# An encoder layer on one core: the first MLP product by seven block products in place of eight

## The chip, the cores and the metric

The kernel runs on one core of a Trainium2 chip. The time is the device time of one execution in microseconds (us), and a version is timed by the median of its runs. PE is the matrix engine (its weight loads, PEld, overlap it), DVE the vector engine, ACT the scalar engine, POOL the general engine; SP issues most DMAs. SBUF is the on-chip memory, PSUM the eight banks into which PE writes.

## The reference

One encoder layer over 1536 tokens (1024 and 512, and 16 meta tokens) of width 1024. After attention, pooling and gates:

```python
x = layer_norm(DEEPNORM_ALPHA * x + mixed, ln1_g, ln1_b)
h = jnp.square(jax.nn.relu(x @ w_mlp1 + b_mlp1))
return layer_norm(DEEPNORM_ALPHA * x + (h @ w_mlp2 + b_mlp2), ln2_g, ln2_b)
```

`w_mlp1` is 1024 x 4096, `w_mlp2` 4096 x 1024, all in fp32. The first MLP product, `x @ w_mlp1`, is what the change computes in another way.

## The kernel before

**Precision.** Each operand of a product is split into a high part in the type fp32r (ACT, `hi`, L120) and the rest (DVE, `lo`, L123). One fp32 product is then three matmuls: high by high, high by rest, rest by high (`three`, L99 to L106; the matmul itself is L97 for the whole kernel). A weight block of 128 x 512 costs one ACT cast and one DVE subtraction.

**Groups.** The tokens are two groups g of 768 (`GN`; six tiles of 128, `GT`; two chunks of 384, `CH`). Phase 1 makes projections and attention. Phase 2 goes, for each group, through the branch projections (`p2`), `out_proj` (L981; PSUM banks added into the accumulator at L1002, statistics at L1003), `ln_N` (normalisation of the six tiles, ACT L193), `ln_T` (PE transposes L1025, ACT scale and shift L1028, split) and `mlp`. Group 0's `ln_T` runs beside group 1's `p2`; then come `out_proj(1)` and the MLPs of both groups.

**First MLP product** (`mlp1_unit`, L1048). A unit m is 128 of the 4096 hidden columns. For each chunk PE runs 8 k-blocks x 3 matmuls of 128x384 into one of six PSUM banks; then ACT takes bias and ReLU (L1060), DVE the square (L1061), ACT the high part, DVE the rest, into `hid`. PE waits for none of that at once: the next chunk has another bank.

**Second MLP product** (`mlp2_half`, L1073). After each four units come two halves of 512 output columns: per token tile 4 x 3 matmuls of 128x512, and one DVE addition to the accumulator (L1070). `residual2` (L1036) multiplies the accumulator by the LN1 row and adds a bias row (DVE L1041) in place. Each group has an accumulator of its own, `acc0` and `acc1`.

**Weights** come from DRAM by SP into three `rawp` buffers of 128x1024 (512 KB a load), are split into two `hlp` buffers, and each load waits until the splits of the buffer's earlier content are done.

**Start.** x is normalised by DVE (L305, L306) with two LN rows, which four small PE matmuls (`psr`) spread over the partitions and ACT copies (L273).

**Order.** The generators in `Background` interleave side work by ticks, one tick after each three matmuls of phase 2. A scheduler then sets the order of each engine's queue; an engine runs its queue strictly in that order, so an instruction that waits holds all behind it.

Of the kernel before, what the change touches and what calls it, by code (L numbers as in the profile page):

```python
# [76 lines left out]
class Trunk:  # L77
# [18 lines left out]
    def mm(self, out, st, mv, start, stop):  # L96
        self.nc.tensor.matmul(out, st, mv, start=start, stop=stop)  # L97

    def three(self, out, sh, sl, mh, ml, first, last, share_st=True):  # L99
        self.mm(out, sh, mh, first, False)  # L100
        self.mm(out, sh, ml, False, False)
        self.mm(out, sl, mh, False, last)
# [42 lines left out]
    def split(self, raw, hl, parts=2, n=D, dst0=0, eng=None):  # L145
        step = n // parts
        for i in range(parts):
            s = slice(i * step, (i + 1) * step)
            d = slice(dst0 + i * step, dst0 + (i + 1) * step)
            self.hi(hl[:, 0, d], raw[:, s])  # L150
            self.lo(hl[:, 1, d], raw[:, s], hl[:, 0, d], eng)
# [96 lines left out]
    def startup(self):  # L248
# [18 lines left out]
        def spread_row(r, n, sel):  # L267

            t = p0.tile([P, D], F32, name=f"row_{n}")
            for i in range(2):  # L270
# [2 lines left out]
                nc.scalar.copy(t[:, i * 512:(i + 1) * 512], ps)  # L273
# [1046 lines left out]
```

## Time and profile before

| | |
|---|---|
| three runs | 2206.4, 2207.15, 2208.91 us; median 2207.15 |
| the profiled execution | 2205.77 us, of which the span is 2204.0 |
| granted PE clock | 0.999 of full |
| PE, PEld | 2176.2 us (99%), 1931.6 us (88%) |
| DVE, ACT, POOL | 1228.2 us (56%), 804.9 us (37%), 155.6 us (7%) |
| first MLP matmul of group 0 | 1130.72 us from the start |

PE is busy when any matmul is in its pipeline. A group's mean time of one matmul (334 ns) is therefore longer than its share of the busy time (538.5 us / 3072 = 175 ns). "Idle before" is the engine's idle time ahead of an instruction, with what ended it.

### The profile page before, as it was taken

The numbers are of one execution on the slowest core, as the hardware profiler recorded it, in microseconds if no ns is written. First come the engines' busy times: TensorE is split into PE (matmuls) and PEld (weight loads), VectorE is DVE, ScalarE is ACT, GpSimd is POOL, SyncE is SP. The second block draws the span as 40 slices with busy tenths as digits, with TensorE's granted clock in tenths as the row PEclk, the third lists the DMA queues.
The fourth block names the chain that finished last, engine by engine and source line by source line (L and its number), as shares of the span: only waits on it lengthen the run. The fifth ranks groups of instructions, "written<-read, shape, count | busy, mean of one in ns | idle before, by whom it ended". The sixth has DMA issues, their size and how long they took to land.

```text
span 2204.0 us, 29394 instructions
## 1 busy us (share of the span) xinstructions
PE 2176.2 (99%) x11216; PEld 1931.6 (88%) x11216; DVE 1228.2 (56%) x2505; ACT 804.9 (37%) x1673; POOL 155.6 (7%) x222
## 2 busy tenths in 40 slices
PE   7999999999999999999999999999999999999998
PEld 6987789887887799799898999999989989989987
DVE  8436678767766536554664433433459443443447
ACT  3235656555554434333323322322332222222221
POOL 3100101101000022120000000000001000000001
PEclk9999999999999999999999999999999999999999
DMA  7342333323322447333323222221223312212211
GB/s 265 126 117 86 93 102 88 100 78 97 90 88 78 134 143 233 107 99 109 128 87 95 68 66 58 69 66 58 69 63 113 91 57 68 68 57 68 67 58 58
DMA packets 124377, 207.42 MB, mean 94 GB/s; under 512 B 23550, under 2 KB 78008, under 8 KB 124236
## 3 DMA queue, kind: packets, MB, share of 16 engines
q1 hardware_dynamic: 121644, 196.11, 29.3%
q0 software_dynamic: 2592, 9.44, 1.2%
q8 instruction: 88, 1.44, 0.3%
q14 instruction: 53, 0.43, 0.1%
HBM read 161.39 MB, written 44.11 MB: 93 GB/s over the span
## 4 chain that ended last, share of the span: by engine, by line
PE 65%; DVE 2%; DMA 1%; ACT 1%; POOL 0%; issue 0%; SPq 0%; DVEq 0%; POOLq 0%; ACTq 0%
PE m L97 48%; PE o L97 6%; PE ya L97 5%; PE psf L97 3%; PE yb L97 2%; PE pt L1025 0%; PE psw L97 0%; DMA gate<-GD 0%; DMA pw<-UT 0%; PE pso L97 0%; DMA oraw<-OT 0%; PE ptt L587 0%; DVE mlo L123 0%; DVE gate L964 0%; ACT S L561 0%
## 5 line engine op out<-in xcount | busy, mean ns | idle before, releaser
L97 PE MATMUL m<-L,hl_w 128*128 128x384 f32 x3072 | 538.5, 334 | 0.5 <-ACT hl_w L120 0.5
L97 PEld LDWEIGHTS m<-L,hl_w 128*128 128x128 f32 x3072 | 534.0, 188 | 3.3 <-ACT hl_w L120 0.9
L97 PE MATMUL m<-hl_w,hid 128*128 128x512 f32 x2304 | 533.6, 390 | 0.3 <-ACT m1f L1060 0.3
L97 PEld LDWEIGHTS m<-hl_w,hid 128*128 128x128 f32 x2304 | 430.5, 188 | 89.1 <-ACT m1f L1060 0.8
L97 PE MATMUL psf<-hT,hl_g 128*128 128x512 f32 x1152 | 306.1, 399 | 0.0
L120 ACT CAST hl_w<-raw_w 128x512 fp32r<-128x512 f32 x256 | 151.3, 619 | 368.1 <-issue 321.2
L1070 DVE TENSOR_TENSOR acc<-acc,m 128x512 f32<-128x512 f32 x192 | 131.3, 685 | 220.2 <-PE m L97 219.9
L97 PEld LDWEIGHTS psf<-hT,hl_g 128*128 128x128 f32 x1152 | 208.3, 189 | 34.1
L1061 DVE TENSOR_TENSOR m1f<-m1f 128x384 f32<-128x384 f32 x128 | 71.4, 559 | 271.4 <-ACT m1f L1060 271.4
L1060 ACT ACTIVATE m1f<-m,cols 128x384 f32<-128x384 f32 x128 | 74.4, 581 | 325.5 <-PE m L97 323.0
L123 DVE TENSOR_TENSOR hl_w<-raw_w,hl_w 128x512 fp32r<-128x512 f32 x256 | 170.4, 690 | 30.1 <-ACT hl_w L120 30.1
L97 PE MATMUL psf<-hT,hl_q 128*128 128x512 f32 x576 | 149.2, 397 | 0.0
L97 PE MATMUL ya<-L,hl_ba 128*128 128x384 f32 x768 | 138.1, 338 | 0.0
L97 PEld LDWEIGHTS ya<-L,hl_ba 128*128 128x128 f32 x768 | 133.6, 188 | 2.4
L561 ACT ACTIVATE S<-S,nm 128x400 f32<-128x400 f32 (+1 forms) x192 | 111.6, 583 | 44.6 <-DVE nm L557 44.5
L97 PE MATMUL o<-hl_wo,mhi 128*128 128x512 f32 x384 | 121.2, 397 | 2.3 <-DVE gate L963 2.1
L97 PEld LDWEIGHTS psf<-hT,hl_q 128*128 128x128 f32 x576 | 105.0, 189 | 17.7
L546 DVE CUSTOM_DVE_ANT_0 S<-pss,base 128x400 f32<-128x400 f32 (+1 forms) x192 | 96.7, 525 | 30.8 <-PE pss L97 30.0
L167 POOL TENSOR_TENSOR rs<-rs,nhalf 128x1 f32<-128x1 f32 (+1 forms) x25 | 34.7, 1388 | 1040.1 <-DVE rs L166 1040.1
L576 POOL TENSOR_SCALAR S<-S,rr 128x400 f32<-128x400 f32 (+1 forms) x96 | 57.3, 609 | 600.2 <-DVE pm L571 511.4
L120 ACT CAST pt<-ptt 128x512 fp32r<-128x512 f32 x128 | 71.4, 582 | 57.6 <-PE ptt L587 57.1
L97 PE MATMUL pss<-kst,qhl 128*128 128x400 f32 (+1 forms) x384 | 88.3, 329 | 1.1 <-DVE qhl L123 0.6
(156 smaller groups left out, 2460.0 us busy)
## 6 DMA issues: line engine op xcount, KB each, us to landing
raw_w<-w_mlp SPq DMA_DIRECT2D x128, 512.0 KB, 3.7
qraw<-QT SPq DMA_DIRECT2D x96, 128.0 KB, 2.7
GD<-eg SPq DMA_DIRECT2D x48, 256.0 KB, 2.3
gate<-GD SPq DMA_DIRECT2D x32, 384.0 KB, 3.1
raw_g<-w_in SPq DMA_DIRECT2D x16, 512.0 KB, 4.6
raw_ba<-w_bo_attn SPq DMA_DIRECT2D x16, 512.0 KB, 3.6
...
```

The costliest lines, as they stand in the source:

```text
L97: self.nc.tensor.matmul(out, st, mv, start=start, stop=stop)
L120: self.nc.scalar.copy(out, in_)
L123: (eng or self.nc.vector).tensor_tensor(out, x, f32(hi), op=ALU.subtract)
L167: self.nc.gpsimd.tensor_tensor(rs, rs, self.nhalf[:rs.shape[0]], op=ALU.pow)
L546: nc.vector.tensor_tensor_reduce(st.S[:, h, :st.n], ps[:, :st.n], self.base[:, st.var, st.o0:st.o0 + st.n], SLOPES[4 * st.j + h], -3.0e38, ...
L561: nc.scalar.activation(st.S[:, h, :st.n], st.S[:, h, :st.n], AF.Exp, bias=nm[:, h:h + 1], accum_out=den[:, h:h + 1])
L576: eng.tensor_scalar(st.S[:, h, :st.n], st.S[:, h, :st.n], rr[:, h:h + 1], 1.0, op0=ALU.mult, op1=ALU.mult)
L1060: nc.scalar.activation(f[:, :CH], ps[:, :CH], AF.Relu, bias=self.cols[:, C_BM1 + m:C_BM1 + m + 1])
L1061: nc.vector.tensor_tensor(f[:, :CH], f[:, :CH], f[:, :CH], op=ALU.mult)
L1070: self.nc.vector.tensor_tensor(ac, ac, ps, op=ALU.add)
```

## The change

**Seven products.** Units p and p+16 become a pair (`pair`). The 1024 input rows, the pair's 256 columns and the 768 tokens are each cut in two, and the 2x2 block product is made by the Winograd form of Strassen's scheme: seven products of 4 k-blocks x 3 matmuls of 128x384 in place of eight. They run in the order B11, T2, T3, T1, B21, T4, B22 into three PSUM banks a, b, c: a, b, c, b, a, c, b; a later product into a bank adds to what stands there. In between the bank is read: after B11 ACT copies a (p1); after T2 DVE makes u2 = b + p1, after T1 u4 = b + p1; then u4 += c (L1172) before T4 adds into c; after T4 u2 += c, and after B22 p1 += b. u4, u2, p1 and bank a (after B21) are the four output blocks; each gets ReLU and square on ACT, and the split.

**Weights of the products** (`w1_ops`). Four of the seven blocks are the weights or combinations of them, made in place in the raw buffers by DVE (s1 = a21 + a22 at L1122, and three more operations), and each of the seven is split into one of four half-size `hlp` buffers. After each product one further split is issued, four products ahead, into the buffer of the product that just ended. The last split of a pair reads the raw buffer of unit p; the load of the next pair's second unit (p+17) goes into that buffer. The second product's weights now have a raw buffer of their own (`raw2`, one).

**Inputs of the products** (`ln_T`). The normalised tiles are stored to DRAM (`XD`) by `ln_N`, read back by column blocks, transposed, and made into seven tiles for each of four k (four subtractions for each k; all 28 split). Group 0's `ln_T` moves into `out_proj(1)`, group 1's into group 0's last second product, at every tick.

**One accumulator.** `out_proj(1)` overwrites it only after group 0's tiles are in `XD`; `residual2` reads `XD`; group 0's sum goes to `ZD`, and its last LN is made in group 1's MLP (`ln2_late`). `ln_N(1)` runs at every second tick from the MLP's start (before: every sixth, 200 ticks later).

**Start.** The two LN rows come by two broadcast DMAs of 512 KB in place of the `psr` matmuls.

In all 2688 matmuls of 128x384 read MLP weights in place of 3072; `psr` goes from 4 to 0; all other matmuls keep their number. ACT has 1792 instructions in place of 1484, DVE 2824 in place of 2508.

**The order on DVE** in group 0 at units 20 and 21 before, and at the pair (8, 24) now. Names: `m_` are PSUM banks (now `m_13357` is b and `m_13358` c), `raw_w_8` and `raw_w_24` the pair's weights, `raw_w_9` and `raw_w_25` the next pair's. Before:

```order
L123 TENSOR_TENSOR hid<-m1f,hid 128x384 [waits Activation_49]
L1061 TENSOR_TENSOR m1f<-m1f 128x384 [waits Activation_49]
L123 TENSOR_TENSOR hl_w_21_13442<-raw_w_21_13253,hl_w_21_13442 128x512 [waits DMAHW1_49,PE_49,Activation_49]
L123 TENSOR_TENSOR hl_w_21_13442<-raw_w_21_13253,hl_w_21_13442 128x512 [waits Activation_49]
L123 TENSOR_TENSOR hid<-m1f,hid 128x384 [waits Activation_49]
L1070 TENSOR_TENSOR acc_8093<-acc_8093,m_13348 128x512 [waits PE_49]
```

and now:

```order
L1170 TENSOR_TENSOR m1f<-m_13357,m1f 128x384 [waits PE_49,Activation_49]
L124 TENSOR_TENSOR hl_w_13390<-raw_w_24_13082,hl_w_13390 128x512 [waits Activation_49]
L124 TENSOR_TENSOR hl_w_13411<-raw_w_8_12926,hl_w_13411 128x512 [waits Activation_49]
L1170 TENSOR_TENSOR m1f<-m_13357,m1f 128x384 [waits PE_49]
L1122 TENSOR_TENSOR s_13453<-raw_w_25_13414 128x512 [waits DMAHW3_49]
L124 TENSOR_TENSOR hl_w_13430<-raw_w_9_13084,hl_w_13430 128x512 [waits DMAHW6_49,Activation_49]
L1172 SCALAR_TENSOR_TENSOR m1f<-m_13358,cols,m1f 128x384 [waits DVE_49]
L1123 TENSOR_TENSOR raw_w_25_13414<-raw_w_9_13084,raw_w_25_13414 128x512 [waits DVE_49]
```

The third row is the pair's last split, which frees the buffer of `raw_w_8`; the fifth waits for the load of `raw_w_25` into that buffer, and u4 += c stands two rows behind it. In 19 of the 31 pairs that have a successor the fifth row's kind stands ahead of L1172 (12 first pairs of a c, 7 second pairs).

**The order on PE** at the same place. Before:

```order
L97 MATMUL m_13432<-L_7807,hl_w_20_13288 128x384 [waits DVE_49]
L97 MATMUL m_13432<-L_7807,hl_w_20_13288 128x384 x23
L97 MATMUL m_13474<-L_7807,hl_w_20_13288 128x384 [waits DVE_49]
L97 MATMUL m_13474<-L_7807,hl_w_20_13288 128x384 x23
L97 MATMUL m_13514<-L_7807,hl_w_21_13442 128x384 [waits DVE_49]
```

and now, from the end of B21 (bank a, `m_13356`) on:

```order
L97 MATMUL m_13356<-XB_11190,hl_w_13373 128x384 x3
L97 MATMUL m_13357<-XB_10774,hl_w_13411 128x384 [waits DVE_49,Activation_49]
L97 MATMUL m_13357<-XB_10774,hl_w_13411 128x384 x2
L97 MATMUL m_13358<-XT_10799,hl_w_13390 128x384 [waits DVE_49]
L97 MATMUL m_13358<-XT_10799,hl_w_13390 128x384 x2
```

Three matmuls of B22 stand ahead of T4, whose first matmul (bank c) waits for DVE, that is, for u4 += c.

**The order on ACT** around group 1's six normalisations. Before:

```order
L120 CAST hid<-m1f 128x384 [waits DVE_49]
L193 ACTIVATE acc_10665<-acc_10665,nmr,rs 128x1024 [waits DMASW6_49]
L193 ACTIVATE acc_10665<-acc_10665,nmr,rs 128x1024 [waits DMASW7_49]
L193 ACTIVATE acc_10665<-acc_10665,nmr,rs 128x1024 [waits DMASW0_49]
L193 ACTIVATE acc_10665<-acc_10665,nmr,rs 128x1024 [waits DMASW1_49,DVE_49]
```

and now, in group 0's first pairs:

```order
L1164 ACTIVATE m1f<-m1f 128x384 [waits Activation_49] x2
L202 ACTIVATE acc<-acc,nmr,rs 128x1024 [waits DMASW4_49,DVE_49]
L202 ACTIVATE acc<-acc,nmr,rs 128x1024 [waits DMASW5_49,DVE_49]
L202 ACTIVATE acc<-acc,nmr,rs 128x1024 [waits DMASW6_49,DVE_49]
L202 ACTIVATE acc<-acc,nmr,rs 128x1024 [waits DMASW7_49,DVE_49]
L202 ACTIVATE acc<-acc,nmr,rs 128x1024 [waits DMASW0_49,DVE_49]
L202 ACTIVATE acc<-acc,nmr,rs 128x1024 [waits DMASW1_49,DVE_49]
L121 CAST hl_w_11449<-raw_w_1_11208 128x512
```

The last row is the split of T2's weights of the second pair; the six normalisations stand ahead of it.

The diff, cut to its core:

```diff
-        self.p_hl = self.pool("hlp", bufs=2)
+        self.p_hl = self.pool("hlp", bufs=4)
...
-            r = self.stage([P, 512], f"r_{n}")
-            nc.sync.dma_start(r[:2, :], a[n].rearrange("(a b) -> a b", b=512))
+            r = p0.tile([P, D], F32, name=f"row_{n}")
+            nc.sync.dma_start(r, a[n].partition_broadcast(P))
...
+        seq2 = []
         for g in range(2):
...
+            for p in range(16):
+                seq += [(f"w1{g}_{p}", a["w_mlp1"][p]), (f"w1{g}_{p + 16}", a["w_mlp1"][p + 16])]
+            for c in range(8):
+                seq2 += [(f"w2{g}_{c}_{h}_{i}", a["w_mlp2"][c, h, i]) for h in range(2) for i in range(2)]
...
+    def raw2_upto(self, i):
+        while self.raw2_n < len(self.seq2) and self.raw2_n <= i:
+            k, src = self.seq2[self.raw2_n]
+            t = self.p_raw2.tile([P, D], F32, tag="raw2", name="raw2")
+            self.nc.sync.dma_start(t, src)
+            self.raw_t[k] = t
+            self.raw2_n += 1
+    def split_w2(self, g, c, h, mk=None):
         for i in range(2):
             key = f"w2{g}_{c}_{h}_{i}"
-            t = self.take(key)
+            n = self.seq2_i[key]
+            self.raw2_upto(n)
+            t = self.raw_t.pop(key)
             for q in range(2):
-                hl = self.p_u.tile([P, 2, 512], F32R, tag="u", bufs=self.NU, name=f"hl_{key}_{q}")
+                hl = mk() if mk else self.u_tile([P, 2, 512], "hl_w2", F32R)
                 self.hl[(g, c, h, 2 * i + q)] = hl
-                run_all(self.split(t[:, q * 512:(q + 1) * 512], hl, 1, n=512))
+                self.split512(hl, t[:, q * 512:(q + 1) * 512])
+                if q == 1:
+                    self.raw2_upto(n + 1)
...
             self.ln_norm(x, x, P, mv[:, t, :], rs[:, t:t + 1])
+            r0 = g * GN + t * P
+            self.nc.gpsimd.dma_start(self.XD[r0:r0 + P], x)
...
+        def load(k, q):
+            x = self.stage([P, 512], "xt")
+            r0 = g * GN + q * CH
+            nc.sync.dma_start(x[:, :CH].rearrange("p (t c) -> p t c", c=P),
+                              self.XD[r0:r0 + CH, k * P:(k + 1) * P].rearrange("(t p) c -> p t c", p=P))
+            return x
+        def turn(x, k):
+            pt = self.ps.tile([P, 512], F32, tag="t", name="pt")
+            for i in range(3):
+                nc.tensor.transpose(pt[:, i * P:(i + 1) * P], x[:, i * P:(i + 1) * P], self.ident)
+            f = self.stage([P, 512], "lnf")[:, :CH]
+            nc.scalar.activation(f, pt[:, :CH], AF.Identity,
+                                 bias=self.cols[:, C_B1 + k:C_B1 + k + 1], scale=self.cols[:, C_G1 + k:C_G1 + k + 1])
+            return f
+        def put(name, k, f):
+            t = self.p_x.tile([P, 2, CH], F32R, tag=f"{name}_{k}", name=f"X{name}{k}")
+            self.hi(t[:, 0], f)
+            self.lo(t[:, 1], f, t[:, 0])
+            self.X[name, k] = t
...
+        xs = [load(0, 0), load(0, 1), load(4, 0)]
+        for k in range(4):
+            xs.append(load(k + 4, 1))
+            yield 1
+            f11 = turn(xs[0], k)
+            yield 1
+            f12 = turn(xs[1], k)
+            yield 1
+            f21 = turn(xs[2], k + 4)
+            yield 1
+            f22 = turn(xs[3], k + 4)
+            if k < 3:
+                xs = [load(k + 1, 0), load(k + 1, 1), load(k + 5, 0)]
+            yield 1
+            put("B11", k, f11)
+            sub(f11, f12, f11)
+            yield 1
+            put("T1", k, f11)
+            sub(f12, f22, f12)
+            yield 1
+            put("T3", k, f12)
+            put("B22", k, f22)
+            sub(f22, f22, f11)
+            yield 1
+            put("T2", k, f22)
+            put("B21", k, f21)
+            sub(f21, f21, f22)
+            yield 1
+            put("T4", k, f21)
...
+    def residual2(self, g):
+        nc = self.nc
+        for t in range(GT):
+            r0 = g * GN + t * P
+            x = [self.stage([P, 512], "xr") for _ in range(2)]
+            for h in range(2):
+                nc.sync.dma_start(x[h], self.XD[r0:r0 + P, h * 512:(h + 1) * 512])
+            yield 1
+            for h in range(2):
+                hs = slice(h * 512, (h + 1) * 512)
+                ac = self.acc[:, t * D + h * 512:t * D + (h + 1) * 512]
+                nc.vector.tensor_tensor(x[h], x[h], self.rows[1][:, hs], op=ALU.mult)
+                nc.vector.tensor_tensor(ac, ac, x[h], op=ALU.add)
...
+    def w1_ops(self):
+        tt = self.nc.vector.tensor_tensor
+        def op(src):
+            t = self.hl_tile("hl_w1")
+            self.split512(t, src)
+            return t
+        for g in range(2):
+            for p in range(16):
...
+                a11, a12, a21, a22 = r0[:, :512], r0[:, 512:], r1[:, :512], r1[:, 512:]
+                yield op(a11)
+                s1 = self.stage([P, 512], "s1")
+                tt(s1, a21, a22, op=ALU.add)
+                tt(a21, a11, a21, op=ALU.subtract)
+                tt(a11, s1, a11, op=ALU.subtract)
+                yield op(a11)
+                yield op(a21)
+                yield op(s1)
+                yield op(a12)
+                yield op(a22)
+                tt(a12, a12, a11, op=ALU.subtract)
+                t = op(a12)
+                self.raw_upto(self.seq_i[k1] + 3)
+                yield t
+    def pull(self):
+        t = next(self.opgen, None)
+        if t is not None:
+            self.ops.append(t)
+    def product(self, bank, name, first=False):
+        w = self.ops.pop(0)
+        for k in range(4):
+            s = slice(k * P, (k + 1) * P)
+            x = self.X[name, k]
+            self.three(bank[:, :CH], w[:, 0, s], w[:, 1, s], x[:, 0], x[:, 1], first and k == 0, k == 3, not first)
+            self.tick()
+        self.pull()
+    def pair(self, g, p):
+        nc = self.nc
+        a, b, c = [self.g_ps("m1") for _ in range(3)]
+        h0, h1 = [self.p_hid.tile([P, 2, GN], F32R, tag="hid", name="hid") for _ in range(2)]
+        self.hids[p], self.hids[p + 16] = h0, h1
+        bias = lambda m: self.cols[:, C_BM1 + m:C_BM1 + m + 1]
+        q0, q1 = slice(0, CH), slice(CH, GN)
+        v = lambda: self.stage([P, 512], "m1f")[:, :CH]
+        def act(f, d, s, src=None, m=None):
+            if src is None:
+                nc.scalar.activation(f, f, AF.Relu)
+            else:
+                nc.scalar.activation(f, src, AF.Relu, bias=bias(m))
+            nc.scalar.activation(f, f, AF.Square)
+            self.hi(d[:, 0, s], f)
+            self.lo(d[:, 1, s], f, d[:, 0, s])
+        def add(o, bank, x, m=None):
+            if m is None:
+                nc.vector.tensor_tensor(o, bank[:, :CH], x, op=ALU.add)
+            else:
+                nc.vector.scalar_tensor_tensor(o, bank[:, :CH], bias(m), x, op0=ALU.add, op1=ALU.add)
+        self.product(a, "B11", True)
+        p1 = v()
+        nc.scalar.copy(p1, a[:, :CH])
+        self.product(b, "T2", True)
+        u2 = v()
+        add(u2, b, p1)
+        self.product(c, "T3", True)
+        self.product(b, "T1")
+        u4 = v()
+        add(u4, b, p1)
+        add(u4, c, u4, p + 16)
+        self.product(a, "B21")
+        f = v()
+        act(f, h0, q0, a[:, :CH], p)
+        act(u4, h1, q1)
+        self.product(c, "T4")
+        add(u2, c, u2, p + 16)
+        act(u2, h1, q0)
+        self.product(b, "B22")
+        add(p1, b, p1, p)
+        act(p1, h0, q1)
...
+        x = self.rows[0][:, h * 512:(h + 1) * 512] if c == 0 else ac
+        self.nc.vector.tensor_tensor(ac, x, ps, op=ALU.add)
...
+    def ln2_late(self):
+        nc = self.nc
+        for t in range(GT):
+            x = [self.stage([P, 512], "z") for _ in range(2)]
+            for h in range(2):
+                nc.sync.dma_start(x[h], self.ZD[t * P:(t + 1) * P, h * 512:(h + 1) * 512])
+            yield 1
+            st = self.p_small.tile([P, 2, 6], F32, tag="st", name="st2")
+            for h in range(2):
+                nc.vector.bn_stats(st[:, h, :], x[h])
+            yield 1
+            self.ln2(0, t, 2, st, x)
...
     def mlp(self, g):
...
+        if g == 1:
+            self.row_load(0, self.ROWD[1])
+            self.row_load(1, self.ROWD[0])
+        for c in range(8):
+            self.want(("w2", g, c, 0), every=10, gen=self.split_w2(g, c, 0))
+            for e in range(2):
+                self.pair(g, 2 * c + e)
+            self.need2(("w2", g, c, 0))
...
+            if c == 7:
+                it = self.bg.add(self.ln_T(1), every=1)
+            sp = self.split_w2(g, c, 1)
+            self.mlp2_half(g, c, 0, sp)
+            for _ in sp:
+                pass
+            self.mlp2_half(g, c, 1)
+            if c == 0:
+                res = self.bg.add(self.residual2(g), every=10)
+            if c == 3 and g == 1:
+                self.bg.finish(res)
+                late = self.bg.add(self.ln2_late(), every=18)
         if g == 0:
...
+            for t in range(GT):
+                self.nc.gpsimd.dma_start(self.ZD[t * P:(t + 1) * P], self.acc[:, t * D:(t + 1) * D])
             self.bg.finish(it)
         else:
...
+            self.bg.finish(late)
...
+        t_it = self.bg.add(self.ln_T(0), every=2)
         self.out_proj(1)
-        self.bg.finish(self.ln_it)
+        self.bg.finish(t_it)
...
+        self.bg.add(self.ln_N(1), every=2)
+        self.ops, self.opgen = [], self.w1_ops()
+        for _ in range(4):
+            self.pull()
```

More of the change, by code (lines that the diff above doesn't have):

```diff
@@ L93, in pool, with mm, three @@
         return self.tc.alloc_tile_pool(**kw)
[L96 to L102, printed above, removed]
+    def mm(self, out, st, mv, start, stop, more=False):
+        self.nc.tensor.matmul(out, st, mv, start=start, stop=stop, skip_group_check=more)
+    def three(self, out, sh, sl, mh, ml, first, last, more=False):
+        self.mm(out, sh, mh, first, False, more)
+        self.mm(out, sh, ml, False, False, more)
+        self.mm(out, sl, mh, False, last, more)
         self.clock += 1
@@ L143, in raw, with split512, split, hl_tile @@
         return t
[L145 to L151, printed above, removed]
+    def split512(self, out, src, eng=None):
+        self.hi(out[:, 0], src)
+        self.lo(out[:, 1], src, out[:, 0], eng)
+    def split(self, raw, hl, eng=None):
+        for i in range(2):
+            self.split512(hl[i], raw[:, i * 512:(i + 1) * 512], eng)
             yield 1
+    def hl_tile(self, name):
+        return self.p_hl.tile([P, 2, 512], F32R, tag="hl", name=name)
     def new_hl(self, key):
-        return self.p_hl.tile([P, 2, D], F32R, tag="hl", name=f"hl_{key}")
+        return [self.hl_tile(f"hl_{key}") for _ in range(2)]
+    def blk(self, w, k):
+        t, s = w[k // 4], slice((k % 4) * P, (k % 4 + 1) * P)
+        return t[:, 0, s], t[:, 1, s]
     def ln_stats(self, x, np_, mv):
@@ L947, in p2 @@
             self.o_it = self.bg.add(self.prep_o(1), every=3)
-        else:
-            self.ln_it = self.bg.add(self.ln_T(0), every=7)
         for m in range(8):
@@ L956, in p2 @@
             ps = [self.g_ps("yb0"), self.g_ps("yb1")]
[L957 to L960 removed]
+            self.fm2(w, (m % 2) * 4, 4, lambda k: self.y(k), ps, cs)
             x = t1.pop(m)
@@ L1086, in mlp2_mm @@
-    def mlp2_mm(self, c, k, t, ws, ps):
-        x = self.hid(4 * c + k)
-        ts = slice(t * P, (t + 1) * P)
-        self.three(ps, x[:, 0, ts], x[:, 1, ts], ws[k][:, 0], ws[k][:, 1], k == 0, k == 3)
-        self.tick()
-    def mlp2_ahead(self, g, c):
-        ws = [self.hl.pop((g, c, 0, i)) for i in range(4)]
         banks = [self.g_ps("m2") for _ in range(GT)]
-        sp = self.split_w2(g, c, 1)
         for k in range(4):
@@ L1100, in mlp2_ahead, with mlp2_mm @@
                 if k == 3:
-                    self.add_acc(g, t, 0, banks[t])
-            next(sp)
-        run_all(sp)
+                    self.add_acc(g, c, t, h, banks[t])
+            if sp is not None:
+                next(sp, None)
+    def mlp2_mm(self, c, k, t, ws, ps):
+        x = self.hid(c, k)
+        ts = slice(t * P, (t + 1) * P)
+        self.three(ps, x[:, 0, ts], x[:, 1, ts], ws[k][:, 0], ws[k][:, 1], k == 0, k == 3)
+        self.tick()
     def mlp2_tile(self, c, t, ws):
```

235 lines of the change are left out of this document (77 added, 158 removed).

## The prediction

> **What bounds the kernel now.** I read the busy shares of the page first, then the chain of waits, then the groups of instructions.
>
> ```profile
> PE 2176.2 (99%) x11216; PEld 1931.6 (88%) x11216; DVE 1228.2 (56%) x2505; ACT 804.9 (37%) x1673; POOL 155.6 (7%) x222
> ...
> PE 65%; DVE 2%; DMA 1%; ACT 1%; POOL 0%; issue 0%; SPq 0%; DVEq 0%; POOLq 0%; ACTq 0%
> ...
> L97 PE MATMUL m<-L,hl_w 128*128 128x384 f32 x3072 | 538.5, 334 | 0.5 <-ACT hl_w L120 0.5
> L97 PE MATMUL m<-hl_w,hid 128*128 128x512 f32 x2304 | 533.6, 390 | 0.3 <-ACT m1f L1060 0.3
> L1070 DVE TENSOR_TENSOR acc<-acc,m 128x512 f32<-128x512 f32 x192 | 131.3, 685 | 220.2 <-PE m L97 219.9
> ```
>
> PE works 99% of the span and waits 0.5 us in all ahead of the first MLP product: PE is the bound, and DVE waits for it (219.9 us at L1070). A matmul of the first product is worth 538.5 / 3072 = 175.3 ns, one of the second 533.6 / 2304 = 231.6 ns. The windows of the stages agree (us; busy time and count of PE, PEld, DVE, ACT, POOL; granted clock; DMA share; GB/s):
>
> ```profile
> 0.00:20.00 20.00, 12.98 (x39) 7.61 (x39) 13.38 (x19) 8.43 (x14) 4.16 (x9) 1.00 0.83 299
> 1190.00:1620.00 430.00, 430.00 (x2190) 392.97 (x2189) 174.46 (x288) 113.87 (x210) 0.00 (x0) 1.00 0.22 64
> 1620.00:1690.00 70.00, 69.46 (x371) 62.28 (x370) 59.95 (x107) 24.32 (x43) 9.82 (x7) 1.00 0.26 91
> 2190.00:2204.00 14.00, 5.16 (x23) 3.94 (x21) 10.60 (x17) 0.00 (x0) 2.49 (x3) 0.81 0.28 112
> ```
>
> In the MLP (second row) PE has no gap, DVE is busy 41%, ACT 26%. So work taken from PE is time, until a new wait appears.
>
> **A. Fewer matmuls.** 3072 - 2688 = 384 of 175.3 ns: **-67.3 us**. All other matmuls stay, but for four `psr` (G).
>
> **B. T4 behind a load.** Before, PE changed banks and waited for nobody. Now T4 adds into bank c, so it needs u4 += c, and on DVE that stands behind s1 of the next pair (L1122), which waits for a load whose buffer the pair's last split frees. The pieces:
>
> ```profile
> 1130.72 19.60 PE L97 MATMUL m<-L,hl_w 128*128 128x384 f32 x112
> 1135.11 0.58 ACT L1060 ACTIVATE m1f<-m,cols 128x384 f32<-128x384 f32 x1 [3.04 <-PE m L97]
> ...
> 1311.01 2.67 ACT L120 CAST hl_w<-raw_w 128x512 fp32r<-128x512 f32 x4 [12.35 <-issue]
> 1311.66 2.05 DVE L123 TENSOR_TENSOR hl_w<-raw_w,hl_w 128x512 fp32r<-128x512 f32 x3 [0.69 <-ACT hl_w L120]
> 1313.07 2.19 SPq L142 DMA_DIRECT2D raw_w<-w_mlp  x2
> ...
> 1144.44 0.56 DVE L123 TENSOR_TENSOR hid<-m1f,hid 128x384 fp32r<-128x384 f32 x1 [0.18 <-ACT hid L120]
> 1144.92 0.68 DVE L123 TENSOR_TENSOR hl_w<-raw_w,hl_w 128x512 fp32r<-128x512 f32 x1
> 1145.52 1.22 DVE L1041 TENSOR_TENSOR acc<-acc,row 128x1024 f32<-128x1024 f32 x1
> ...
> L1061 DVE TENSOR_TENSOR m1f<-m1f 128x384 f32<-128x384 f32 x128 | 71.4, 559 | 271.4 <-ACT m1f L1060 271.4
> ...
> 12.72 1.28 DVE L306 SCALAR_TENSOR_TENSOR x<-x,rs,row_b 128x1024 f32<-128x1024 f32 x1 [0.68 <-ACT row_b L273]
> ...
> 14.06 1.97 PE L312 MATMUL pt<-ident,x 128*128 128x128 f32 x8 [2.06 <-DVE x L306]
> ...
> DMA to landing us min/median/max: 3.4/3.6/4.5
> ```
>
> From the end of T3 (time 0; it frees the last split's buffer): PE to ACT 0.19 (24 matmuls from 1130.72 end at 1134.92, ACT starts at 1135.11); ACT's start to DVE's 0.65 (1311.01, 1311.66); the subtraction 0.69 (2.05 / 3), SP's issue 0.05 later: 1.58. Landing 3.4 to 4.5 (last row, the weight loads of the first MLP); I take 3.8, above the median since the second load of a pair issued together is the late one: 5.38. Then s1 and one split's subtraction at DVE's pace of 0.60 (1144.92 to 1145.52), u4 += c at 0.55 (as L1061), and 0.06 to PE (14.06, where the operation from 12.72 ends at 14.00): **7.19 us**. Meanwhile PE has T1 and B21, 12 matmuls or 2.10 us each, and of B22 what stands ahead of T4: 3 matmuls (0.53) in first pairs of a c, 5 (0.88) in second ones. Stall 7.19 - 4.73 = 2.46 us in 12 pairs, 7.19 - 5.08 = 2.11 in 7: **+44.3 us** for the 19 pairs of this order. With landings of 3.4 and 4.5 it is 36.7 and 57.6. In the other 12 pairs u4 += c comes first: T1's end 2.10 + 0.19 + two operations of 0.55 to 0.69 + splits between them stay under 4.2, nothing is lost.
>
> **C. The first two pairs of group 0.**
>
> ```profile
> 1127.52 1.37 DVE L1002 SCALAR_TENSOR_TENSOR acc<-acc,o 128x512 f32<-128x512 f32 x2 [2.81 <-PE o L97]
> ...
> 1134.76 1.21 DVE L1041 TENSOR_TENSOR acc<-acc,row 128x1024 f32<-128x1024 f32 x1
> ...
> L193 ACT ACTIVATE acc<-acc,nmr,rs 128x1024 f32<-128x1024 f32 x12 | 14.0, 1230 | 0.0
> L120 ACT CAST hid<-m1f 128x384 fp32r<-128x384 f32 x128 | 65.6, 513 | 49.0 <-DVE m1f L1061 49.0
> ```
>
> The last additions and statistics of `out_proj(1)` hold DVE for 7.24 us (1127.52 to 1134.76), 4 of them after the MLP's start; before, nobody needed DVE then. Now B21 and T1 wait for its subtractions and sums: about 1 to 2 us. The six normalisations now stand on ACT ahead of the split of the second pair's T2: 6 x 1.23 = 7.4 us. Before, only a `hid` and a later weight stood behind them. B11's 2.1 us and one matmul group hide part; their statistics also wait behind s1 on DVE. I take 7 us there and 5 for the rest (copy and u2 behind it, PSUM banks freed late): **+12** (7 to 17).
>
> The Trainium skill ("TensorE: Matmul & The Clock Gate", section "HAM oscillation — how this bites in real kernels") allows "no PE-idle gaps >~3.4µs", after which PE runs at half clock. Of the gaps above only C's is longer; by that rule the 3.4 us behind it are worth half, +1.7 us as an estimate. This trace has a gap of 2.06 us at 14.06 with a granted clock of 1.00; no gap over 3.4 us inside the work is seen.
>
> **D. Inputs of group 1's products.** `ln_T(1)` runs at every tick of two halves of the second product: 48 triples x 3 x 0.2316 = 33.4 us.
>
> ```profile
> L1028 ACT ACTIVATE lnf<-pt,cols 128x384 f32<-128x384 f32 x32 | 21.4, 669 | 25.2 <-PE pt L1025 21.3 <-DVE st L162 2.1 <-ACT lnf L1028 1.8
> L123 DVE TENSOR_TENSOR L<-lnf,L 128x384 fp32r<-128x384 f32 x32 | 17.8, 555 | 0.5
> L123 DVE TENSOR_TENSOR hl_w<-raw_w,hl_w 128x512 fp32r<-128x512 f32 x256 | 170.4, 690 | 30.1 <-ACT hl_w L120 30.1
> ```
>
> DVE gets 28 splits and 16 subtractions at 0.48 (1144.44 to 1144.92) to 0.555, 8 weight splits and 12 additions at 0.60 to 0.69: 33 to 38 us, as long as PE. Below nothing it can't be; if DVE ends last, 5 us, and 10 if the stage buffers hold the next column block too. I take **+5** (0 to 10). **E.** `ln_T(0)` at every second tick of `out_proj(1)`, 96 ticks x 0.69 = 67 us, has twice the time: +1 (0 to 5).
>
> **F. Through DRAM.** `XD` is written once and read twice, `ZD` written and read: 25 MB over some 1000 us, 25 GB/s on top of 64 (second window), DMA busy 0.22. Only the 3 MB store of `ZD` beside group 1's first loads, and that group's first addition behind it, touch PE: 3 MB at the 299 GB/s of the first window is 10.5 us, mostly under the first pairs: **+4** (0 to 10).
>
> **G. Start.**
>
> ```profile
> 4.39 1.29 DVE L162 BATCH_NORM_STATS2 st<-x 128x6 f32<-128x512 f32 x2 [4.39 <-DMA x<-x_prompt]
> ...
> 9.57 2.46 DVE L305 SCALAR_TENSOR_TENSOR x<-x,mv,row_g 128x1024 f32<-128x1024 f32 x2
> ```
>
> x arrives at 4.39, its statistics end at 5.7, and the row g is what L305 waits for until 9.57. By DMA the row could be there at about 6; but 1 MB more goes through DMAs that are busy 83% at 299 GB/s, 3.5 us. Both signs: **-1.5** (-3 to +2). **H. End.** One raw buffer for the last second product: +0.5 (0 to 2); PE has 12 tiles of 2.8 us to hide it.
>
> **Extra ACT and DVE work.** Per pair DVE has 7 splits, 4 combinations, 6 sums and 4 rests, about 12 us under PE's 84 x 0.1753 = 14.7 us; ACT less. It costs nothing while the order lets it run beside PE; where not, it is B or the second rival.
>
> **Sum.** -67.3 + 44.3 + 12 + 5 + 1 + 4 - 1.5 + 0.5 = -2.0 us on the profiled execution of 2205.77: 2203.8. The median of the runs lies 1.4 above it: **2205.2 us**. With all bounds at their lower end -26.6 (2180.5), at their upper end +36.3 (2243.5). The forecast's own range is 2192 to 2218.
>
> **Rivals.**
>
> *The load is not late.* If the freed buffer's load lands before u4 is due, or DVE's order turns out otherwise, B is nothing: 2205.2 - 44.3 = 2160.9. For it: DMA is busy 0.22. Against: the load can't be issued before 1.58 us after T3, and would have to land in under 1.4; no row has less than 3.4. Chance 0.14, that other buffers or an earlier free make the chain shorter than I read it.
>
> *The second pairs' T1 waits for u2 (slower).* In each c's second pair, from B11's end: 2.10 + 0.19, then on ACT in order a split cast (0.62), a square and the copy p1 (0.58 each), a `hid` cast (0.51) and a split cast (0.62), then on DVE a subtraction (0.69) and u2 (0.56): 6.45, 0.06 to PE: 6.5. T1 is due after 36 + 2 matmuls, 6.66. The slack is 0.15 us. If each of the six hand-overs inside it costs 0.19 us, as PE to ACT does, T1 is 1 us late; with B22's end and its ReLU late as well I price 1.4 us in 16 pairs: +22, 2227 us. It decides from 0.03 us a hand-over. For it: the profiled rows follow each other on one engine closer than their durations. That speaks as much against it, since 1144.92 to 1145.52 is less than 0.68. Chance 0.20.
>
> *The clock falls.* Each of B's 19 gaps could bring what the last window shows, a granted clock of 0.81 over 14 us: 14 x 0.19 = 2.7 us each, +51, 2256. For it: that window is one in which PE stands idle. Against: PE is busy there 5.16 of 14 us, in B it would be some 12 of 14.5, and the gap of 2.06 us at 14.06 lies in a window at 1.00. Chance 0.05. The Trainium skill's rule above, with its 3.4 us, speaks against it too.
>
> *Everything hides.* B at its short landing and C to H at their lower ends: 2180.5. Chance 0.09.
>
> **How the numbers follow.** The forecast has 0.52. A measurement of this kernel can tell 0.2% from no change: 2202.7 to 2211.6. Of the forecast's own spread I give 0.20 below, 0.21 within and 0.11 above it. Faster: 0.20 + 0.14 + 0.09 = 0.43; same 0.21; slower 0.11 + 0.20 + 0.05 = 0.36. The range reaches from 2175, which takes in the last rival and leaves out the first, to 2235, which takes in the second and leaves out the third.
>
> **What would show it.** A: the group of 128x384 matmuls, 2688 of them, at 471 us busy. B: on DVE, waits at L1122 for `raw_w`, and on PE 19 waits for L1172 of 2 to 2.5 us, PE's share at about 97%. C: PE gaps of about 7 us within 40 us of the MLP's start. D and F: gaps around the change of groups. If T4 shows no waits, B was wrong; if T1 in second pairs waits for L1170, the slower rival is right; a clock under 1.00 in the MLP's windows speaks for the third.

## The result

| | before | changed |
|---|---|---|
| median of the runs, us | 2206.78 (four) | 2152.14 (four, 2151.95 to 2152.56) |
| ratio | | 0.9751, 95% interval 0.9734 to 0.9768 |
| profiled execution, its span | 2205.77, 2204.0 | 2152.28, 2150.5 |
| first MLP matmul starts at | 1130.72 | 1124.19 |
| first to last MLP matmul | 1064.05 | 1017.14 |

The change makes the kernel 54.6 us (2.5%) faster. 2205.2 us had been predicted, with a range of 2175 to 2235; the time lies below the range.

The busy shares, the chain of waits and two groups of the page of the changed kernel:

```profile
PE 2113.6 (98%) x10824; PEld 1867.6 (87%) x10824; DVE 1402.1 (65%) x2821; ACT 955.8 (44%) x1981; POOL 162.6 (8%) x240
...
PE 86%; DVE 5%; DMA 4%; ACT 2%; issue 1%; SPq 0%; POOL 0%; DVEq 0%; ACTq 0%; POOLq 0%
...
L97 PE MATMUL m<-XT,hl_w 128*128 128x384 f32 x1536 | 285.5, 339 | 8.9 <-DVE m1f L1172 4.5 <-ACT hl_w L121 3.7
L97 PE MATMUL m<-XB,hl_w 128*128 128x384 f32 x1152 | 215.8, 335 | 1.3 <-DVE m1f L1170 0.9 <-ACT hl_w L121 0.4
```

PE is still the bound. DVE has 174 us more to do (65% in place of 56%), and PE's waits for it and for ACT ahead of the first product grew from 0.5 to 10.2 us. The two groups' busy times add up to 501.3 us, but they overlap: where a group's last matmul and the next group's first are both in the pipeline, the time counts in both. Start to start the 2688 matmuls take 489.6 us, against 535.8 us for 3072 before, that is 174.4 ns each before and 182.1 now.

Where the 53.5 us between the two spans come from (starts of matmuls in the two traces; the prediction's letters behind):

| stretch | before | changed | difference |
|---|---|---|---|
| start to the first matmul of attention's projections (G) | 104.03 | 100.48 | -3.55 |
| from there to the branch projections | 676.12 | 673.54 | -2.58 |
| from there to the first MLP matmul (E) | 350.57 | 350.17 | -0.40 |
| first to last MLP matmul (A, B, C, D, F) | 1064.05 | 1017.14 | -46.91 |
| rest (H) | 9.23 | 9.18 | -0.05 |

And in the MLP: 384 matmuls fewer at 174.4 ns are -67.0. In the first product PE's starts come later than its 173.3 ns rhythm by 21.7 us in all (delays over 0.03 us; pairs are counted 0 to 31, from 16 on in group 1): 6.7 us in group 0's first two pairs (0 and 1), 4.1 in group 1's first pair (16), 3.2 in the pairs 2 and 18, 7.7 in the 27 others together. The second product lost nothing (520.4 against 521.2 us).

The list of PE's waits of the changed kernel (waited for: us in total, times, longest):

```profile
PE pt L312 <- DVE x L306: 11.5, 1, 11.5
PE m L97 <- DVE m1f L1172: 4.5, 7, 2.3
PE m L97 <- ACT hl_w L121: 4.1, 2, 3.7
...
PE m L97 <- DVE m1f L1170: 0.9, 2, 0.6
```

The wait for u4 += c (L1172), which the prediction priced at 44 us, is there, but with 4.5 us. Its cause, s1's wait for the load, reads so in the answer for line 1122 from 1150 us on (its engine sat idle before it):

```profile
L1122 DVE TENSOR_TENSOR s<-raw_w x30: 680/691/694, 1157.1 to 2088.4; 128x512 f32<-128x512 f32 x30
...
  DMA raw_w<-w_mlp: 5.4, 13
```

The same place that the prediction's section B worked out, pair (8, 24) of group 0, in the timeline of the changed kernel:

```profile
1383.39 6.40 PE L97 MATMUL m<-XT,hl_w 128*128 128x384 f32 x36
...
1386.33 0.69 DVE L124 TENSOR_TENSOR hl_w<-raw_w,hl_w 128x512 fp32r<-128x512 f32 x1
1387.05 2.41 SPq L143 DMA_DIRECT2D raw_w<-w_mlp  x2
1387.75 0.62 ACT L121 CAST hl_w<-raw_w 128x512 fp32r<-128x512 f32 x1 [1.46 <-PE m L97]
1388.41 0.69 DVE L124 TENSOR_TENSOR hl_w<-raw_w,hl_w 128x512 fp32r<-128x512 f32 x1 [1.39 <-ACT hl_w L121]
...
1390.49 0.69 DVE L1122 TENSOR_TENSOR s<-raw_w 128x512 f32<-128x512 f32 x1
1391.10 0.68 DVE L124 TENSOR_TENSOR hl_w<-raw_w,hl_w 128x512 fp32r<-128x512 f32 x1
1391.70 0.61 DVE L1172 SCALAR_TENSOR_TENSOR m1f<-m,cols,m1f 128x384 f32<-128x384 f32 x1
...
1392.37 1.83 PE L97 MATMUL m<-XT,hl_w 128*128 128x384 f32 x9
```

T2 starts at 1383.39 and ends at 1385.47, T3 ends at 1387.55. The load for s1 is issued at 1387.05, half a microsecond before T3's end, and not 1.58 us behind it: it follows the last split but one (1386.33 to 1387.02, of `raw_w_24`), not the last (1388.41, of `raw_w_8`). In the built program `raw_w_25` does stand at the SBUF address of `raw_w_24`: of the three buffers the next tile gets the one that comes free first. The words ahead of the prediction and its section B, which say that the load goes into the buffer of unit p, are wrong in this. The load lands after 3.4 us, as s1's turn comes, and T4 starts 0.24 us late.

### The profile page after: what moved, and what is told of

It is laid out like the page before. It is cut to its first block, busy times and chain, and to the rows that moved or that the text cites. A ratio compares the mean times of both kernels' runs of the same rounds, so it can differ in the third digit from the quotient of the medians.

```text
span 2150.5 us, 29495 instructions
## 1 busy us (share of the span) xinstructions
PE 2113.6 (98%) x10824; PEld 1867.6 (87%) x10824; DVE 1402.1 (65%) x2821; ACT 955.8 (44%) x1981; POOL 162.6 (8%) x240
## 4 chain that ended last, share of the span: by engine, by line
PE 86%; DVE 5%; DMA 4%; ACT 2%; issue 1%; SPq 0%; POOL 0%; DVEq 0%; ACTq 0%; POOLq 0%
PE m L97 39%; PE psf L97 20%; PE o L97 6%; PE ya L97 4%; PE pso L97 3%; PE yb L97 3%; PE pss L97 3%; PE ptt L587 2%; PE psv L97 2%; DMA raw_w<-w_mlp 2%; PE psk L97 2%; DVE hl_w L124 1%; DMA gate<-GD 1%; ACT S L561 1%; ACT hl_w L121 1%
## 5 line engine op out<-in xcount | busy, mean ns | idle before, releaser
L97 PE MATMUL m<-XT,hl_w 128*128 128x384 f32 x1536 | 285.5, 339 | 8.9 <-DVE m1f L1172 4.5
L97 PEld LDWEIGHTS m<-XT,hl_w 128*128 128x128 f32 x1536 | 268.4, 189 | 18.2 <-DVE m1f L1172 11.5
L121 ACT CAST hl_w<-raw 128x512 fp32r<-128x512 f32 x128 | 79.5, 622 | 347.5 <-DMA raw<-w_mlp 200.2
L97 PE MATMUL m<-XB,hl_w 128*128 128x384 f32 x1152 | 215.8, 335 | 1.3 <-DVE m1f L1170 0.9
L97 PEld LDWEIGHTS m<-XB,hl_w 128*128 128x128 f32 x1152 | 202.0, 188 | 3.5 <-issue 1.5
L121 ACT CAST hl_w<-raw_w 128x512 fp32r<-128x512 f32 x192 | 118.1, 619 | 140.7 <-PE m L97 118.1
L124 DVE TENSOR_TENSOR hl_w<-raw_w,hl_w 128x512 fp32r<-128x512 f32 x192 | 131.5, 688 | 64.0 <-ACT hl_w L121 63.3
L124 DVE TENSOR_TENSOR hl_w<-raw,hl_w 128x512 fp32r<-128x512 f32 x128 | 88.1, 690 | 129.4 <-ACT hl_w L121 128.6
L1202 DVE TENSOR_TENSOR acc<-acc,m 128x512 f32<-128x512 f32 x168 | 106.2, 682 | 83.7 <-PE m L97 83.4
```

The source lines that it names most:

```text
L97: self.nc.tensor.matmul(out, st, mv, start=start, stop=stop, skip_group_check=more)
L121: self.nc.scalar.copy(out, in_)
L124: (eng or self.nc.vector).tensor_tensor(out, x, f32(hi), op=ALU.subtract)
L1202: self.nc.vector.tensor_tensor(ac, x, ps, op=ALU.add)
```

## The experiments

**1. Is the order itself dear?** Control for the next run. u4 += c is made to depend on s1 in the 19 pairs in which it stands behind it, so that no rescheduling changes the order (`LATE` lists the 19).

```diff
-                yield op(a11)
-                s1 = self.stage([P, 512], "s1")
+                early = 16 * g + p - 1 in LATE
+                t = op(a11)
+                if not early:
+                    yield t
+                s1 = self.s1 = self.stage([P, 512], "s1")
                 tt(s1, a21, a22, op=ALU.add)
+                if early:
+                    yield t
...
-        add(u4, c, u4, p + 16)
+        if 16 * g + p in LATE:
+            bt = self.p_small.tile([P, 1], F32, tag="bt", name="bt")
+            nc.vector.scalar_tensor_tensor(bt, self.s1[:, :1], 0.0, bias(p + 16), op0=ALU.mult, op1=ALU.add)
+            nc.vector.scalar_tensor_tensor(u4, c[:, :CH], bt, u4, op0=ALU.add, op1=ALU.add)
+        else:
+            add(u4, c, u4, p + 16)
```

> Control for the next run: in the 19 pairs in which s1 of the next pair already stands ahead of u4 += c on DVE, u4 += c is made to depend on s1 (its bias is first added to 0 times one column of s1, one small DVE operation), so that the order cannot change; the loads are as in the changed kernel. Theory 1 (the buffer of the pair's second unit, free one product earlier than the prediction had it, takes the load, so s1 hardly waits): 2152 + 19 x 0.3 to 0.9 us for the small operation and s1 standing ahead of u4 = b + p1 too, 2155 to 2170. Rival (s1 is not on PE's path at all): 2152 to 2154.

Measured: 2155.89 us (0.9768 of before, 0.9753 to 0.9782), 3.8 us over the changed kernel, but the two intervals overlap, and in the traces the MLP takes 1017.29 us against 1017.14. The order by itself, with the load one product early, costs nothing that the MLP shows.

**2. The price of the late load.** As 1, and the two loads that follow a pair change places in the list of weights, so that s1's load takes the buffer of the last split.

```diff
-            for p in range(16):
-                seq += [(f"w1{g}_{p}", a["w_mlp1"][p]), (f"w1{g}_{p + 16}", a["w_mlp1"][p + 16])]
+        us = [[(f"w1{g}_{p + o}", a["w_mlp1"][p + o]) for g in range(2) for p in range(16)] for o in (0, 16)]
+        seq += [us[0][0], us[1][0], us[0][1]]
+        for n in range(1, 32):
+            seq += us[0][n + 1:n + 2] + [us[1][n]]
...
-                self.raw_upto(self.seq_i[k1] + 3)
+                self.raw_upto(self.seq_i[k1] + (3 if g + p == 0 else 2))
```

> As the control, but with the order of two loads exchanged, so that the load that s1 waits for takes the buffer that the pair's last split frees, as the prediction had it: one product (2.1 us) later. Theory 1: the prediction's price was right for this order and only the buffer was misread; T4 waits 2 to 2.5 us more in each of the 19 pairs, 38 to 48 us over the control; and if each gap of over 2 us halves PE's clock for a while, as after the one gap of 2.42 us in the changed kernel (10 matmuls 0.15 us longer), 1.5 us more in each, 66 to 76 in all. Rival (the price itself was wrong: landing or hand-overs shorter than read): less than 15 us over the control.

Measured: 2165.89 us (0.9816, 0.9802 to 0.9831), 10.0 us over the control (12.0 in the MLP of the two traces): far under theory 1, within what the rival gave, but not for the rival's reason. The timeline at pair (8, 24) shows why:

```profile
1383.90 6.40 PE L98 MATMUL m<-XT,hl_w 128*128 128x384 f32 x36
...
1387.55 2.41 SPq L144 DMA_DIRECT2D raw_w<-w_mlp  x2
...
1388.91 0.69 DVE L125 TENSOR_TENSOR hl_w<-raw_w,hl_w 128x512 fp32r<-128x512 f32 x1 [1.39 <-ACT hl_w L122]
1390.14 4.15 PE L98 MATMUL m<-XB,hl_w 128*128 128x384 f32 x23
...
1393.68 0.69 DVE L1128 TENSOR_TENSOR s<-raw_w 128x512 f32<-128x512 f32 x1 [2.00 <-DMA raw_w<-w_mlp]
...
1394.89 1.49 PE L98 MATMUL m<-XB,hl_w 128*128 128x384 f32 x7 [0.60 <-DVE m1f L1178]
...
1395.42 0.61 DVE L1195 SCALAR_TENSOR_TENSOR m1f<-m,bt,m1f 128x384 f32<-128x384 f32 x1
...
1396.22 1.03 PE L98 MATMUL m<-XT,hl_w 128*128 128x384 f32 x5
```

T3 ends at 1388.06 (24 matmuls of the 36 from 1383.90). The second of the two loads (1389.63) is s1's: 1.57 us behind T3's end, where the prediction had 1.58. It lands at 1393.68, after 4.05 us (prediction: 3.8), and u4 += c ends at 1396.03, 7.97 us behind T3's end. The prediction's chain gave 7.19 to PE's start; the difference is the landing's 0.25 and the operations that the edit puts between (u4 = b + p1, 0.46, and the small one, 0.07). So the chain and its price were right for this buffer. But the scheduler's order for PE is another one here: 11 matmuls of the next pair's first product (23 in place of 12 in the row at 1390.14) and seven of B22 stand ahead of T4, so that PE lost about 1 us and not 2.5, most of it ahead of B22, which waits for u4 = b + p1 behind the same s1. What a late operand costs in one order can't be carried to another.

**3. Take the wait away.** u4 is summed in another order, so that bank c is read before DVE comes to s1.

```diff
         self.product(c, "T3", True)
-        self.product(b, "T1")
         u4 = v()
-        add(u4, b, p1)
-        add(u4, c, u4, p + 16)
+        add(u4, c, p1, p + 16)
+        self.product(b, "T1")
+        add(u4, b, u4)
```

> u4 is made in the other order: u4 = c + p1 + bias after T3, and u4 += b after T1. T4's bank is then read before DVE reaches s1. Theory 1: the small gaps at T4 (0.1 to 0.5 us each, about 7 us in all outside the first pair of a group) and the gap of 2.4 us with 1.5 us at half clock in group 1's first pair go: 2152 - 7 to 11 = 2141 to 2145. Rival (DVE as a whole is late there, and the wait moves to B22 or to T1 of the next pair): 2149 to 2153.

Measured: 2140.58 us (0.9699, 0.9684 to 0.9713), 11.6 us under the changed kernel, and no wait for L1172 is left:

```profile
PE m L97 <- ACT hl_w L121: 4.2, 1, 4.2
PE m L97 <- DVE m1f L1170: 3.5, 3, 1.5
```

The first is group 0's second pair (experiment 4), the second T1 in three pairs (experiments 7 to 9). The 11.6 us are a net figure. By the starts in the two traces the pairs other than 1, 3, 17 and 19 lose 16.1 us less, group 1's first pair and the pairs 2 and 18 among them, and T1 in the pairs 3, 17 and 19 loses 4.2 us more. So all that the waits for u4's two additions cost in the changed kernel is at most 16 us, little more than a third of the 44 us predicted for L1172 alone.

**4. The six normalisations** (C). They start 30 ticks later, one at every fourth tick.

```diff
-        self.bg.add(self.ln_N(1), every=2)
+        self.bg.add(self.ln_N(1), every=4, delay=30)
```

> The six normalisations of group 1 start 30 ticks later and come at every fourth tick, among the second pair's work. Theory 1 (they stood on ACT ahead of the split of T2's weights, 3.9 us and then 2 us at half clock): both go, 2152 - 4 to 6 = 2146 to 2148. Rival (the work only moves, and second product's additions then wait for the accumulator's stores): 2150 to 2156.

Measured: 2146.06 us (0.9726, 0.9709 to 0.9742), 6.1 us less. What goes is this, in the changed kernel's timeline:

```profile
1137.97 6.90 ACT L202 ACTIVATE acc<-acc,nmr,rs 128x1024 f32<-128x1024 f32 x6
...
1144.77 0.60 ACT L121 CAST hl_w<-raw_w 128x512 fp32r<-128x512 f32 x1
...
1145.43 6.38 PE L97 MATMUL m<-XT,hl_w 128*128 128x384 f32 x24 [3.71 <-ACT hl_w L121]
```

Six normalisations hold ACT for 6.9 us, and the cast of T2's weights behind them comes so late that PE stands for 3.71 us. The excess over PE's rhythm in the pairs 0 and 1 falls from 6.7 to 0.06 us.

**5. The start** (G). The four spreading matmuls again, all else as in the changed kernel.

```diff
-            r = p0.tile([P, D], F32, name=f"row_{n}")
-            nc.sync.dma_start(r, a[n].partition_broadcast(P))
+            r = self.stage([P, 512], f"r_{n}")
+            nc.sync.dma_start(r[:2, :], a[n].rearrange("(a b) -> a b", b=512))
...
+                self.mm(ps, sel[:2, i], r[:2, :], True, True)
+                nc.scalar.copy(t[:, i * 512:(i + 1) * 512], ps)
```

> The two LN rows are spread by four PE matmuls again, all else as in the changed kernel. Theory (the start alone gave the 3.6 us by which attention begins earlier in the changed kernel's trace, 100.48 us against 104.06): 2152 + 3 to 4 = 2155 to 2156, first transposes at 14 us. Rival (the start gave less, and the half-size weight buffers the rest): 2152 to 2153.5.

Measured: 2156.59 us (0.9777, 0.9761 to 0.9794), 4.5 us more. In the trace the transposes start at 14.03 again (11.52 in the changed kernel) and attention's projections at 103.98 (100.48; 99.5 to 102.0 in the experiments with the new start). Part of it is taken back before the MLP, which starts 1.8 us later; the profiled execution is 2.6 us longer. The 2.6 us that the changed kernel gains within attention are still there (673.63 us), so they are not the start's; what in the change gives them stays open.

**6. Both orders together**, the edits of 3 and 4.

> u4's other order and the later normalisations together. Theory (two separate waits): 2152 - 11.6 - 6.1 = 2134 to 2136, left over the gaps at T1 in the pairs 3, 17 and 19, 4.4 us together. Rival (one has hidden part of the other): 2137 to 2141.

Measured: 2135.16 us (0.9678, 0.9664 to 0.9693), as the two add up: they were separate waits. 4.8 us over PE's rhythm are left, all in T1 of the pairs 3, 17 and 19.

**7. Group 0's stores in halves** (F), on 6: the columns of one half of the second product go to DRAM while the other is computed.

```diff
+            if c == 7:
+                self.store_z(0)                # the first 512 columns of the six tiles
             self.mlp2_half(g, c, 1)
...
-                self.nc.gpsimd.dma_start(self.ZD[t * P:(t + 1) * P], self.acc[:, t * D:(t + 1) * D])
+            self.store_z(1)
```

> As e6, and group 0's sum is stored to DRAM in two halves, each after its half of the second product, in place of 3 MB at once beside group 1's first loads. Theory (the load of group 1's second pair, landing after 5.7 us in place of 3.5, is late because of these stores): the gap of 1.7 us at group 1's second pair falls to under 0.5, 1 to 2 us less than e6. Rival (the load is late for other traffic, or first product's own loads): same as e6.

Measured: 2134.79 us (0.9675, 0.9661 to 0.9690), not to be told from 6. The gap in pair 17 is gone, and another is there in its place:

```profile
PE m L97 <- DVE m1f L1170: 2.7, 2, 1.4
...
PE pt L1043 <- DMA xt<-XD: 1.2, 1, 1.2
```

The load for pair 17's s1, which is made in pair 16, lands after 3.61 us in place of 5.92 in 6: the stores had made it late. The earlier stores now meet the column blocks that `ln_T(1)` reads. So the stores are the cause of pair 17's gap; moving them only moves it.

**8. The residual's reads earlier**, on 7: two `yield`s between read and use in place of one.

> As e7, and each read of a normalised tile for the residual stands 20 ticks ahead of its use in place of 10. Theory (DVE waits at the residual's multiplication for a read that is 5 to 6 us under way, and u2 or u4 stands behind it): the gaps of 1.0 to 1.4 us at T1 in the pairs 3 and 19 go, 2 us less than e7. Rival (it is DVE's own work there): same as e7.

Measured: 2132.93 us (0.9672, 0.9658 to 0.9687). The gaps stay: 1.75 us in pair 3, 1.15 in pair 19 (1.59 and 1.42 in 7). The difference of 1.9 us to 7 is therefore not theirs; the intervals overlap, and in this trace the MLP starts 1.9 us earlier. But the run does not decide between theory and rival, because the wait for the read stays too. DVE's waits for `xr`, first in 7, then here:

```profile
DVE xr L1098 <- DMA xr<-XD: 2.6, 2, 1.4
...
DVE xr L1099 <- DMA xr<-XD: 2.6, 2, 1.6
```

They stand in the pairs 2 and 18, at each group's first tile, whose read is issued 2.5 us into the pair in both traces; the edit moved only what comes behind it.

**9. The residual elsewhere**, on 6: its DVE operations among the second product's matmuls.

```diff
-            if c == 0:
-                res = self.bg.add(self.residual2(g), every=10)
+            if c == 1:                         # ahead of the first half of the second product
+                res = self.bg.add(self.residual2(g), every=2)
```

> As e6, and the residual's 24 DVE operations of a group come in the two halves of the second product of c = 1 (at every second tick) in place of at every tenth tick from c = 1's first pair on. Theory (they stand in the DVE queue between the steps that lead to u2 of the second pair, whose chain has hardly any slack, and delay T1): the gaps of 1.7 and 1.2 us at T1 in the pairs 3 and 19 go, 2135.2 - 2 to 3.2 = 2132 to 2133. Rival (the gaps there have another cause, a read under way): 2135.

Measured: 2132.15 us (0.9659, 0.9643 to 0.9675), the lowest median of all, though the intervals of 6 to 9 overlap; the MLP takes 996.4 us in place of 999.7 in 6. The gaps in the pairs 3 and 19 are gone; of 4.8 us over PE's rhythm 1.3 are left, all in pair 17:

```profile
PE m L97 <- DVE m1f L1170: 1.0, 1, 1.0
```

DVE's wait for `xr` is gone as well. So the residual was the cause of the two gaps; whether by DVE's own operations or by the wait for the first read in the pairs 2 and 18 stays open.

**10. How much slack has u2?** On 6; in second pairs u2 = b + p1 is computed twice.

```diff
         add(u2, b, p1)
+        if p % 2:
+            add(u2, b, p1)
```

> As e6, and in every second pair of a c u2 = b + p1 is computed twice, so that PE's T1 is released one DVE operation (0.48 us at DVE's pace) later. Theory (u2 ends 0.7 to 1.4 us ahead of T1 in this kernel's second pairs, other than in the changed kernel, where it ends 0.05 us ahead in six of them): most of it is hidden, 2135 to 2137; only the pairs 3, 17 and 19, where T1 waits for u2 already, lose 0.5 us each. Rival (second pairs have no slack at all, as the prediction's slower case had it): 16 x 0.5 = 8 us, 2143.

Measured: 2140.48 us (0.9698, 0.9684 to 0.9713), 5.3 us more: between the two. First pairs lose nothing; the ordinary second pairs lose 0.1 to 0.7 us each (4.4 us in 13 pairs), and the pair 17 2.7 us more. Their slack is smaller than the 0.7 to 1.4 us that I read from the ends of u2, but it isn't zero.

## Why the prediction was wrong

**The bound and A: right.** PE bounds both kernels, and 384 matmuls fewer are -67.0 us at the measured rhythm (predicted: -67.3).

**B: the step that failed**, +44.3 predicted. The mechanism is there (s1 waits for its load in 13 pairs, 5.4 us; PE waits for L1172, 4.5 us), and the price of the chain held when the load was made as late as assumed (7.97 us against 7.19 plus the inserted operations). What was wrong is its first row: the load was taken to follow the pair's last split. It follows the last but one, one product (1386.33 to 1388.41, 2.08 us) earlier. 7.19 - 2.08 is 5.11, which leaves 0.4 us of stall in first pairs and 0.03 in second ones. Measured at T4 are 0.0 to 0.6 us in each of 18 of the 19 pairs, 5.8 us together, and 4.1 in pair 16, where the load is late for another reason (F). The three buffers had been counted through in rotation; the program hands out the buffer that is free first. That could have been seen before the result, in the addresses of the two tiles. The first rival ("that other buffers or an earlier free make the chain shorter than I read it") named this and had 0.14; its 2160.9 is the nearest of the times given.

**C: right in kind, too high.** +12 (7 to 17) against 6.7 measured, just under its range, of which about 2 us are matmuls at half rate. The normalisations' 6.9 us on ACT were right; the 5 us for "the rest" were 0.7.

**D: no cost.** +5 (0 to 10) predicted; the second product takes 520.4 us, with `ln_T(1)` in it. DVE ended in time. **E:** +1 predicted, -0.4 measured for the whole stretch, which takes 348.4 to 351.9 us in the experiments' traces, so that this is within the spread. **H:** nothing.

**F: right.** +4 (0 to 10). The stores make the load that pair 16 waits for land after 5.7 us (3.6 where they come in halves, experiment 7); PE then loses 2.42 us and 1.5 more at half rate:

```profile
1643.35 2.41 SPq L143 DMA_DIRECT2D raw_w<-w_mlp  x2
...
1649.08 0.69 DVE L1122 TENSOR_TENSOR s<-raw_w 128x512 f32<-128x512 f32 x1 [2.39 <-DMA raw_w<-w_mlp]
...
1650.95 2.47 PE L97 MATMUL m<-XT,hl_w 128*128 128x384 f32 x8 [2.26 <-DVE m1f L1172]
```

That the 4.1 us come so near to 4 is luck, as the half rate was not in the term. The pairs 2 and 18 (3.2 us) were not in the sum: there the residual's operations stand on DVE ahead of u4's two additions, and the first of them waits 2.94 us (2.64 in pair 18) for its read:

```profile
1201.40 0.69 DVE L1098 TENSOR_TENSOR xr<-xr,row 128x512 f32<-128x512 f32 x1 [2.94 <-DMA xr<-XD]
```

**G: right in sign, too small.** -1.5 (-3 to +2) predicted, -3.5 measured at attention's start. The row is there when the statistics are, and x times g starts at 6.09:

```profile
6.09 1.28 DVE L305 SCALAR_TENSOR_TENSOR x<-x,mv,row_ln_emb_g 128x1024 f32<-128x1024 f32 x1
...
11.52 3.67 PE L312 MATMUL pt<-ident,x 128*128 128x128 f32 x16 [11.52 <-DVE x L306]
```

**The slower rival** (u2 too late in second pairs): its chain was right to 0.1 us. In seven second pairs (7, 9, 11, 13, 15, 23, 31) u2 ends 6.54 us behind the pair's start (predicted 6.45), and T1 starts at 6.60 (6.66). The hand-overs cost what the rows say and hardly more: T1's second matmul starts 0.11 us late in each, 0.8 us in all in place of 22.

**The clock.** It does fall, behind two gaps, which costs 3.5 us in all. Behind B's 18 gaps, of at most 0.6 us, no such slow stretch follows. Windows of the changed kernel around the two longest gaps of its MLP (the granted clock is the third number from the end):

```profile
1144.00:1146.00 2.00, 0.57 (x2) 0.30 (x2) 0.59 (x1) 2.00 (x4) 1.06 (x2) 1.00 1.00 387
1146.00:1150.00 4.00, 3.89 (x14) 3.85 (x14) 3.03 (x7) 4.00 (x10) 0.00 (x0) 0.57 0.72 281
1150.00:1154.00 4.00, 4.00 (x25) 3.96 (x24) 3.89 (x7) 2.20 (x6) 0.00 (x0) 1.00 0.18 16
1648.00:1651.00 3.00, 0.74 (x6) 0.42 (x4) 1.92 (x4) 0.65 (x2) 0.00 (x0) 1.00 0.44 178
1651.00:1655.00 4.00, 4.00 (x14) 4.00 (x15) 2.82 (x5) 2.97 (x7) 0.00 (x0) 0.57 0.00 0
1655.00:1659.00 4.00, 4.00 (x25) 4.00 (x24) 2.79 (x5) 2.83 (x7) 0.00 (x0) 1.00 0.00 0
```

In the 4 us window behind each gap PE has 14 matmuls in place of 25. The Trainium skill ("TensorE: Matmul & The Clock Gate", section "HAM oscillation — how this bites in real kernels") has PE at half clock after idle gaps of over some 3.4 us; the first gap agrees, but the second is 2.26 us of idle, so here the measurement decides, and the limit lies lower. The gap of 2.06 us at 14.06 in the kernel before does not speak against a falling clock, as the prediction had it: the eight transposes behind it take 1.97 us, eight of the same kind at 21.36 take 1.10, though the windows' clock shows 1.00 for both. What slows the first eight is not shown.

```profile
21.36 1.10 PE L312 MATMUL pt<-ident,x 128*128 128x128 f32 x8 [1.48 <-DVE x L306]
```

**The sum.** Against -2.0 predicted stand -53.5 measured. B was 38.5 us too high (44.3 against 5.8; pair 16 stands with F), C, D and E together 12, G 2; 2.6 us in attention and the 3.2 in the pairs 2 and 18 had no term. All but the last went the same way, towards faster. The 11 us for C's "rest", D and E had been put in without a chain of rows that ends at PE; 0.7 us of them were there.
